# Expert products of a mixture layer: from split weights on the whole array to plain float32 on column quarters

## The chip, the cores and the metric

The kernel runs on one core of one Trainium2 chip. The metric is the device time of one execution in microseconds, from the first to the last instruction with what lies around it. All times in this document are of that one core. The engines are named as the profile names them: PE is TensorE (PEld its weight loads, PEldq its sequencer), ACT is ScalarE, DVE is VectorE, POOL is GpSimd and SP is SyncE, which here issues nearly all transfers.

## What is computed

A two-layer encoder trunk on 256 tokens of width 1024 in float32. Each layer has a mixer of four branches, a layer norm, a feed-forward part and another layer norm. The feed-forward part of the first layer is a dense SwiGLU; that of the second is a mixture of 8 experts, of which each token uses its two best. Everything that the change touches lies in that mixture:

```python
def swiglu(x, w1, w3, w2):
    return (jax.nn.silu(x @ w1) * (x @ w3)) @ w2

def moe_swiglu(x, router, w1, w3, w2):
    logits = jnp.einsum('bsd,de->bse', x.astype(jnp.float32), router.astype(jnp.float32))
    top_logit, top_idx = lax.top_k(logits, TOP_K)
    top_w = jax.nn.softmax(top_logit, axis=-1)
    gate = jnp.sum(jax.nn.one_hot(top_idx, N_EXPERTS, dtype=jnp.float32) * top_w[..., None], axis=-2)
    gate = gate.astype(x.dtype)
    out = jnp.zeros_like(x)
    for e in range(N_EXPERTS):
        out = out + gate[..., e:e + 1] * swiglu(x, w1[e], w3[e], w2[e])
    return out
```

An expert's w1 and w3 are 1024 x 3584 and its w2 is 3584 x 1024, so the eight experts have 352 MB of weights, and each is read once. The result has to hold float32 accuracy.

## The kernel before

The kernel sends only the tokens of an expert through it. The router (L716 to L743) takes the logits of all tokens, the two best experts of each, and the place of each token in each of its experts. A one-hot matrix of places times the tokens (`gather`, L805) gives `xe`, the tokens of two experts at a time, 128 places each. An expert that has more than `CAP` = 128 tokens would be finished in a second pass behind the branch at L959, which these inputs don't take.

Products are made in a fast format that holds less than float32. So each operand is split into a high and a low part: ScalarE copies a half block of weights into the fast format (`high`, L134), VectorE subtracts that from the original (`low`, L138), and `mm3` (L165) adds three products: high by high, high by low, low by high. The tokens are the stationary operand, 128 at a time, and the weights stream past them 512 columns wide, always over the full array of 128 x 128.

The weights come in blocks of 1 MB, 42 for each expert: 28 with columns of w1 and w3 side by side, 14 with rows of w2. SP fetches them (`fetch`, L114, the transfer at L118) into a ring of 15 places. The order of the 336 blocks is `order` (L635): two blocks of w1 and w3, which give 256 hidden columns, then the w2 block that belongs to the hidden columns two units earlier. Fourteen blocks are asked for ahead of the router, and three more ahead of the load of the count (below).

The loop over blocks is `steps` (L919), and the program order on each engine is written by hand: a step issues a block's 12 products (`first` for w1 and w3, `second` for w2), then SwiGLU (`act`, L587 and L588), then the split of the halves of later blocks (`half`), then what is due (`at`): the turn of a hidden chunk by two transposes (L845) and its split (L162, L163), the add of the finished expert (L878 to L880, one-hot places times results, scaled by the gate and added to `acc`), and the gather of the next two experts (L811). The accumulators are four banks `mm` for first products, gathers and adds, two banks `s` for second products, and two `tr` for turns. The count of the fullest expert (`over`, L897) is loaded to all engines ahead of the loop. The final norm (L216 to L232) and the output (L987) follow.

Elsewhere in the kernel, at L471 in the latent attention, products are made in plain float32, with 32 tokens on each of four quarters of the array's columns.

Of the kernel before, what the change touches and what calls it, by code (L numbers as in the profile page):

```python
# [36 lines left out]
LAG = 2  # L37
NW = 5
NR2 = 2
# [33 lines left out]
def trunk(tc, A, out):  # L73
# [8 lines left out]
    lnp = pool("ln", bufs=1)  # L82
    zp = pool("z", bufs=1)
# [24 lines left out]
    xh = cst.tile([128, 2, 8, 128], F32R, name="xh")  # L108
    xl = cst.tile([128, 2, 8, 128], F32R, name="xl")
# [18 lines left out]
    class Split:  # L128
# [3 lines left out]
        def high(self, raw, h):  # L132
            self.w.append([wp.tile([128, 1024], F32R, name=k)[:, :self.n] for k in ("wh", "wl")])
            nc.scalar.activation(self.w[h][0], raw[:, h * self.n:(h + 1) * self.n], AF.Copy)  # L134
# [500 lines left out]
    order = []  # L635
    for j in range(FFE // 256 + LAG):
        order += [2 * j, 2 * j + 1] * (j < FFE // 256) + [28 + j - LAG] * (j >= LAG)
    moe_raw = []

    def moe_fetch(n):  # L640
        return fetch(A["wmoe"][0, order[n]], zp, f"z{n}")

    def moe(xs, gb):
        with tc.tile_pool(name="moe", bufs=1, reuse_waits="tile") as ep:
            nj = FFE // 256
# [4 lines left out]
            places = [(zp, f"z{n}", None) for n in range(NZ)] + [(rawp, "raw", None)] * 4 + [(ep, "raw2", NR2)] * NR2  # L650
            first_places = list(places)
            places[1:1] = [(lnp, "gb", None), (xp, "x", None)]
            ring = len(places)

            def prefetch(i, p, tag, n):
                ready[0, order[i]] = fetch(src[0, order[i]], p, tag, n)

            def block(e, i):

                if (e, i) in ready:  # L660
                    return ready.pop((e, i))
                late = e * NU + order.index(i) - NE * NU
                if places[count[0] % ring][1] == "gb" and late > -36:
                    count[0] += 1
                raw = fetch(src[e, i], *places[count[0] % ring], parts=2 if late >= -2 else 1)
                count[0] += 1
                return raw

            for n in range(NZ, ring - 2):
                prefetch(n, *first_places[n])  # L670
            prefetch(len(first_places), ep, "ey", None)
            for n in range(NZ):
                ready[0, order[n]] = moe_raw[n]
            first_parts = []

            steps = [(e, i) for e in range(NE) for i in order]
            raws, parts = {}, {}

            def high(n, h):
                if h == 0:  # L680
                    raws[n], parts[n] = block(*steps[n]), Split()
                parts[n].high(raws[n], h)

            def low(n, h, eng=None):
                parts[n].low(raws[n], h, eng)

            def half(q, eng=None):

                high(q // 2, q % 2)
                low(q // 2, q % 2, eng)  # L690
# [8 lines left out]
            xT = ep.tile([128, 2, 8, 128], F32, name="rxT", tag="xe")  # L699
# [8 lines left out]
            flat = lambda a, t: a[:, t].rearrange("p k c -> p (k c)")  # L708
# [13 lines left out]
            def by_token(t):  # L722
                lgT = ep.tile([NE, 128], F32, name="lgT", tag="fs", bufs=2)
# [21 lines left out]
            def places_of(e, off, oh=None, ts=(0, 1)):  # L745

                oh = ep.tile([128, 2, 256], F32R, name="ohe") if oh is None else oh
                for t in ts:
                    for i in range(2):
                        nc.vector.tensor_scalar(oh[:, t, i * 128:(i + 1) * 128], iota, off + 1.0,  # L750
                                                pos[:, t, e + i:e + i + 1], op0=ALU.add, op1=ALU.is_equal)
                return oh

            pw = mm.tile([128, 512], F32, name="mm")
# [3 lines left out]
            half(0)  # L758
            for t in range(2):
                xs.begin(t)  # L760
            high(0, 1)
            high(1, 0)
            x.append(xs(0))
            x.append(xs(1))
            scopy(flat(xh, 0), x[0])
# [3 lines left out]
            nc.vector.tensor_tensor(flat(xl, 0), x[0], f(flat(xh, 0)), op=ALU.subtract)  # L769
            two(0, lg0)  # L770
            spin(pw[:, 0:128], 2)
            place(0)
            oh = places_of(0, 0, ts=(0,))
            scopy(flat(xh, 1), x[1])
            lg1 = by_token(1)
            low(0, 1)
            spin(pw[:, 0:128], 2)
            two(1, lg1)
            spin(pw[:, 0:128], 2)
            place(1)  # L780
            places_of(0, 0, oh, (1,))
            nc.vector.tensor_tensor(flat(xl, 1), x[1], f(flat(xh, 1)), op=ALU.subtract)
            low(1, 0)
            for q in range(3, NW):
                half(q)
            for t in range(2):
                nc.scalar.mul(x[t], x[t], ALPHA)
# [5 lines left out]
            acc = x  # L793
            sums = ep.tile([128, 2, 2], F32, name="sums")

            def weights(*_):
                nc.vector.tensor_scalar(w1, w2, 1.0, None, op0=ALU.add)
                nc.vector.reciprocal(w1, w1)
                nc.vector.tensor_tensor(w2, w2, w1, op=ALU.mult)
                for t in range(2):  # L800
# [346 lines left out]
```

## Time and profile before

| | us |
|---|---|
| median of 3 runs (lowest, highest) | 1680.96 (1678.39, 1681.54) |
| the profiled execution | 1681.01 |
| its span, first to last instruction | 1678.9 |
| of it up to the router | 657 |
| router and first gather | 21 |
| experts | 982 |
| last add, final norm, output | 18 |

One page of the profile sums up one execution: busy time of each engine, a picture of the span in 40 slices, queues, waits and the costliest groups of instructions. "Busy" of TensorE is modelled from pipelined records. A product in plain float32 leaves two weight loads and two MATMUL records, one in the fast format a single pair. [...] A row of waits names the engine and tile that waited, and what came last. The views behind the router are the ones that matter here.

### The profile page before, as it was taken

The numbers are of one execution on the slowest core, as the hardware profiler recorded it, in microseconds if no ns is written. First come the engines' busy times: TensorE is split into PE (matmuls) and PEld (weight loads), VectorE is DVE, ScalarE is ACT, GpSimd is POOL, SyncE is SP. The second block draws the span as 40 slices with busy tenths as digits, with TensorE's granted clock in tenths as the row PEclk, the third lists the DMA queues.
The fourth block names the chain that finished last, engine by engine and source line by source line (L and its number), as shares of the span: only waits on it lengthen the run. The fifth ranks groups of instructions, "written<-read, shape, count | busy, mean of one in ns | idle before, by whom it ended". The sixth has DMA issues, their size and how long they took to land. (4 is left out here: it accounts for less than half of the span.)

```text
span 1678.9 us, 21171 instructions
## 1 busy us (share of the span) xinstructions
PE 1648.5 (98%) x7783; PEld 1332.3 (79%) x7783; DVE 1380.9 (82%) x1834; ACT 1112.1 (66%) x1466; POOL 25.7 (2%) x29
## 2 busy tenths in 40 slices
PE   8999999999999999999999999999999999999996
PEld 7687878888868787888888888888888888888884
DVE  7688585554868858898988989998989988989986
ACT  4556645443455664777777777777777777777774
POOL 1000000000100000000000000000000000000000
PEclk9999999999999999999999999999999999999998
DMA  9344546555544655899999899999999999999860
GB/s 348 136 150 171 185 169 209 176 179 197 191 169 155 238 190 191 332 332 373 353 369 350 337 370 370 354 356 352 351 366 363 345 378 342 350 369 369 345 245 27
DMA packets 66928, 467.99 MB, mean 279 GB/s; under 512 B 7552, under 2 KB 8192, under 8 KB 11264
## 3 DMA queue, kind: packets, MB, share of 16 engines
q1 hardware_dynamic: 66816, 466.55, 74.8%
q8 instruction: 63, 1.03, 0.3%
q14 instruction: 49, 0.40, 0.1%
HBM read 465.48 MB, written 1.05 MB: 278 GB/s over the span
## 5 line engine op out<-in xcount | busy, mean ns | idle before, releaser
L138 DVE TENSOR_TENSOR wl<-raw,wh 128x1024 fp32r<-128x1024 f32 x870 | 1015.8, 1217 | 196.9 <-ACT wh L134 192.4
L134 ACT ACTIVATE wh<-raw 128x1024 fp32r<-128x1024 f32 x870 | 879.6, 1053 | 234.8 <-PE mm L170 201.4
L170 PE MATMUL mm<-wh,xe 128*128 128x512 f32 x1792 | 525.7, 397 | 0.0
L170 PEld LDWEIGHTS mm<-wh,xe 128*128 128x128 f32 x1792 | 328.5, 188 | 67.4
L170 PE MATMUL s<-wh,eh 128*128 128x512 f32 x896 | 299.8, 396 | 0.0
L170 PE MATMUL mm<-wl,xe 128*128 128x512 f32 x896 | 278.8, 392 | 0.0
L170 PEld LDWEIGHTS s<-wh,eh 128*128 128x128 f32 x896 | 168.7, 188 | 38.7
L170 PEld LDWEIGHTS mm<-wl,xe 128*128 128x128 f32 x896 | 168.1, 188 | 37.9
L587 ACT ACTIVATE fs<-mm 128x256 f32<-128x256 f32 x134 | 51.6, 385 | 206.7 <-PE mm L170 206.7
L170 PE MATMUL mm<-wh,xh 128*128 128x512 f32 (+2 forms) x592 | 183.2, 390 | 2.1 <-ACT xh L162 2.1
L170 PE MATMUL mm<-wh,xl 128*128 128x512 f32 (+2 forms) x592 | 179.2, 386 | 0.0
L170 PE MATMUL mm<-wl,xh 128*128 128x512 f32 (+2 forms) x592 | 178.6, 384 | 0.0
L170 PE MATMUL s<-wl,eh 128*128 128x512 f32 x448 | 177.0, 395 | 0.0
L170 PEld LDWEIGHTS mm<-wh,xh 128*128 128x128 f32 x592 | 108.5, 189 | 25.3 <-ACT xh L162 4.1
L170 PEld LDWEIGHTS mm<-wl,xh 128*128 128x128 f32 x592 | 109.2, 189 | 22.5 <-issue 0.8
L170 PEld LDWEIGHTS mm<-wh,xl 128*128 128x128 f32 x592 | 108.2, 189 | 22.1 <-issue 1.5
L170 PEld LDWEIGHTS s<-wl,eh 128*128 128x128 f32 x448 | 84.6, 189 | 18.8
L588 DVE TENSOR_TENSOR fs<-mm,fs 128x256 f32<-128x256 f32 x134 | 56.7, 423 | 36.2 <-ACT fs L587 35.9
L519 DVE SCALAR_TENSOR_TENSOR ac<-ud,smc,ac 128x256 f32<-128x256 f32 x120 | 53.2, 480 | 0.7
L163 DVE TENSOR_TENSOR eh<-tr,eh 128x256 fp32r<-128x256 f32 x112 | 46.8, 418 | 0.0
L162 ACT ACTIVATE eh<-tr 128x256 fp32r<-128x256 f32 x112 | 41.2, 368 | 4.5 <-PE tr L845 4.2
L845 PE MATMUL tr<-ident,fs 128*128 128x128 f32 x224 | 42.6, 272 | 0.0
(212 smaller groups left out, 1187.5 us busy)
## 6 DMA issues: line engine op xcount, KB each, us to landing
raw<-wmoe SPq DMA_DIRECT2D x334, 1024.0 KB, 6.4
raw<-wpre SPq DMA_DIRECT2D x95, 1024.0 KB, 4.9
gb<-lnp SPq DMA_DIRECT2D x5, 1024.0 KB, 5.8
raw<-wpre SPq DMA_DIRECT2D x4, 704.0 KB, 5.8
z<-biasB SPq DMA_DIRECT2D x8, 256.0 KB, 2.7
raw<-wmoe SPq DMA_DIRECT2D x4, 512.0 KB, 7.2
z<-cw SPq DMA_DIRECT2D x2, 640.0 KB, 6.6
x<-x SPq DMA_DIRECT2D x2, 512.0 KB, 3.9
```

Source lines behind the costliest of these rows:

```text
L134: nc.scalar.activation(self.w[h][0], raw[:, h * self.n:(h + 1) * self.n], AF.Copy)
L138: (eng or nc.vector).tensor_tensor(wl, raw[:, h * self.n:(h + 1) * self.n], f(wh), op=ALU.subtract)
L162: nc.scalar.activation(hi, src, AF.Copy)
L163: (eng or nc.vector).tensor_tensor(lo, src, f(hi), op=ALU.subtract)
L170: nc.tensor.matmul(ps, o[i], o[j], start=start and q == 0 and k == 0, stop=stop and q == 2 and k == n - 1)
L519: later.append(lambda c=c, k=k, w=w: nc.vector.scalar_tensor_tensor(ac[:, c], ud[:, c, k:k + S], w(k), ac[:, c], op0=ALU.mult, op1=ALU.add))
L587: nc.scalar.activation(s, ps[:, 0:256], AF.Silu)
L588: nc.vector.tensor_tensor(s, ps[:, 256:512], s, op=ALU.mult)
L845: nc.tensor.transpose(tr[:, i], s[:, i * 128:(i + 1) * 128], ident)
```

## The change

The experts' products are made in plain float32, so the weights need no split. The tokens of an expert are cut into tiles of 32. A tile is the stationary operand of one quarter of the array's columns, and the weights stream past it. Four chunks of 512 columns (256 of w1 and 256 of w3) are handled at once, one on each quarter: `quad(0)` to `quad(2)` of 8 blocks each, and `quad(3)` of 4 blocks with two chunks, so that two tiles share a bank. `second(q)` spreads the second products over the quarters in a like way, by the table `TASKS`. The order of blocks changes to match: first all of a quad, later its w2 blocks, and the last two w2 blocks of an expert behind the first eight of the next.

How many tiles an expert has is known only on the chip. The router counts the tokens of each expert (`cnt`), makes a class of 0 to 3 of it (`arm`: over 32, over 64, over 96), and TensorE loads the eight classes as registers. `arms` then writes each set of products four times, for 1 to 4 tiles, and two compares choose one. Only TensorE branches on the class. There are six sets for each expert. Banks without a tile get zeros by a product with a zero matrix, so that the other engines do the same work for any class. The products of a block wait for that block inside the arm; a place of the ring comes free when the arm has run its last products.

The gather is made for one expert at a time in float32. `acc` is a tile of its own. The ring has 21 places. Fifteen of its blocks are asked for ahead of the load of the count, which all engines make behind the router, and the rest behind it.

```diff
+            places = [(zp, f"z{n}", None) for n in range(NZ)] + [(rawp, "raw", None)] * 4
+            places += [(xhp, "xh", None), (xhp, "xl", None)]
+            places += [(wp, "w", None)] * NW + [(ep, "raw2", NR2)] * NR2
+            early = NZ + 4
...
+            order = []
+            for e in range(NE):
+                order += [(e, n) for n in range(8)] + [(e - 1, n) for n in (40, 41) if e]
+                order += [(e, n) for n in range(8, 40)]
+                order += [(e, n) for n in (40, 41) if e == NE - 1]
...
+            nc.vector.tensor_copy(cnt, pc)
+            nc.vector.tensor_scalar(arm, cnt, 32.5, None, op0=ALU.is_gt)
+            for c in (64.5, 96.5):
+                nc.vector.scalar_tensor_tensor(arm, cnt, c, arm, op0=ALU.is_gt, op1=ALU.add)
+            nc.vector.tensor_copy(armi, arm)
...
+            _, sel = nc.values_load_multi_w_load_instructions(armi[0:1, 0:NE], engines=[PE], min_val=0, max_val=3)
+            over = nc.values_load(mosti[0:1, 0:1], min_val=0, max_val=S)
...
+                        def body(b):
+                            for fn in fns:
+                                fn(b)
+                        v = sel[self.e]
+                        with tc.If(v < 2) as c:
+                            with tc.If(v < 1) as d:
+                                body(1)
+                            with d.Else():
+                                body(2)
+                        with c.Else():
+                            with tc.If(v < 3) as d:
+                                body(3)
+                            with d.Else():
+                                body(4)
...
+                def quad(self, q, lo=0, hi=8):
+                    def products(b):
+                        for k in range(lo, hi):
+                            if q < 3:
+                                w = self.w[8 * q + k]
+                                todo = [(self.ps[q][r][32 * c:32 * c + 32], r, w[:, c * 512:(c + 1) * 512])
...
+                            for ps, r, wc in todo:
+                                nc.tensor.matmul(ps, self.xe[:, k, 32 * r:32 * r + 32], wc, start=k == 0, stop=k == 7)
...
+                for e in range(NE + 1):
+                    x_ = None
+                    if e < NE:
+                        x_ = Expert(e, oh, xe)
+                        x_.blocks(*range(8))
+                        x_.quad_places(0)
+                        x_.arms(x_.quad(0))
+                    if last:
+                        last.blocks(40, 41)
+                        last.arms(last.second(3))
+                        last.evacuate()
+                    if e == NE:
+                        break
+                    x_.act(0)
+                    if e + 1 < NE:
+                        oh = places_of(e + 1, 0)
+                    x_.blocks(*range(8, 16))
+                    x_.quad_places(1)
+                    x_.turn_places(0)
+                    x_.arms(x_.quad(1))
+                    x_.turn(0)
+                    x_.turned(0)
+                    x_.act(1)
+                    if last:
+                        last.add()
+                    x_.second_places()
+                    x_.blocks(*range(16, 24), *range(28, 32))
+                    x_.quad_places(2)
+                    x_.turn_places(1)
+                    x_.arms(x_.quad(2), x_.second(0))
+                    x_.turn(1)
+                    x_.turned(1)
+                    x_.act(2)
+                    if e + 1 < NE:
+                        xe = gather(oh)
+                    x_.blocks(*range(24, 28), *range(32, 36))
+                    x_.quad_places(3)
+                    x_.turn_places(2)
+                    x_.arms(x_.quad(3), x_.second(1))
+                    x_.turn(2)
+                    x_.turned(2)
+                    x_.act(3)
+                    x_.blocks(*range(36, 40))
+                    x_.turn_places(3)
+                    x_.where_places()
+                    x_.turn(3)
+                    x_.turned(3)
+                    x_.arms(x_.where, x_.second(2))
+                    x_.wheres()
+                    if e == NE - 1:
                         gt = gb()
-                ex[NE - 1].add((0, 0), (0, 1))
+                    last = x_
+                last.add((0, 0), (0, 1))
 
                 with tc.If(over > CAP):
```

On TensorE, a unit of three blocks stood as this in the program before: products of two blocks of w1 and w3, of one of w2 (`s`), with a turn (`tr`) among them.

```order
L170 MATMUL s<-wl,eh 128x512
L170 MATMUL s<-wh,eh 128x512 x2
L170 MATMUL s<-wl,eh 128x512
L170 MATMUL s<-wh,eh 128x512
L170 MATMUL mm<-wh,xe 128x512 x2
L170 MATMUL mm<-wl,xe 128x512 x2
L170 MATMUL mm<-wh,xe 128x512 x4
L170 MATMUL mm<-wl,xe 128x512 x2
L170 MATMUL mm<-wh,xe 128x512 x2
L845 MATMUL tr<-ident,fs 128x128 x2
L170 MATMUL mm<-wh,xe 128x512 x2
L170 MATMUL mm<-wl,xe 128x512 x2
```

Now the same engine comes to `quad(0)` of the first expert so, behind the gather (L788): the load of the classes, two compares, and all four arms behind each other (32, 64, 96 and 128 products; `zero` fills the idle banks).

```order
L788 MATMUL tr<-oh,x 128x128 x16
L848 TENSOR_LOAD armi
L877 COMPARE_AND_BRANCH
L878 COMPARE_AND_BRANCH
L908 MATMUL mm<-raw,xe 32x512 x4
L913 LDWEIGHTS zero
L913 MATMUL mm<-zero 128x512
L913 LDWEIGHTS zero
L913 MATMUL mm<-zero 128x512
L913 LDWEIGHTS zero
L913 MATMUL mm<-zero 128x512
L908 MATMUL mm<-raw,xe 32x512 x28
```

These are the compares and the arm for one tile. The end of the same set, from the products of the arm for two tiles on, stands so, and the next set follows:

```order
L908 MATMUL mm<-raw,xe 32x512 x56
L878 UNCONDITIONAL_BRANCH
L883 COMPARE_AND_BRANCH
L908 MATMUL mm<-raw,xe 32x512 x12
L913 LDWEIGHTS zero
L913 MATMUL mm<-zero 128x512
L908 MATMUL mm<-raw,xe 32x512 x84
L883 UNCONDITIONAL_BRANCH
L908 MATMUL mm<-raw,xe 32x512 x128
L883 UNCONDITIONAL_BRANCH
L848 ISA x16
L877 COMPARE_AND_BRANCH
```

What stood as 12 products for each block, one after the other, is now a choice of four stretches that lie behind each other, of which three are jumped over.

On SP, which issues the transfers, the fetches of blocks (`wmoe`) around the router stood so, with the load of the count (`mosti`) behind three of them:

```order
L118 DMA raw<-wpre 128x2048 x9
L118 DMA raw<-wmoe 128x2048 x7
L694 DMA rt<-router 128x64
L118 DMA raw<-wmoe 128x2048 x3
L897 TENSOR_LOAD mosti
L897 ISA x2
L118 DMA raw<-wmoe 128x2048 x303
```

Now the load stands behind seven:

```order
L118 DMA raw<-wmoe 128x2048
L721 DMA rt<-router 128x64
L118 DMA raw<-wmoe 128x2048 x7
L849 TENSOR_LOAD mosti
L849 ISA x2
L118 DMA raw<-wmoe 128x2048
L877 UNCONDITIONAL_BRANCH
L118 DMA raw<-wmoe 128x2048 x4
L877 UNCONDITIONAL_BRANCH
L118 DMA raw<-wmoe 128x2048 x13
```

With the eight that stand further up, 15 blocks are asked for ahead of the load, where it was 17; the fetches behind it are cut by a jump at the end of each set, one for each set of arms (L877).

## Rows read from the trace of the kernel before

**Rows 1.** the page's first part: busy us, share of the span, instructions

```profile
PE 1648.5 (98%) x7783; PEld 1332.3 (79%) x7783; DVE 1380.9 (82%) x1834; ACT 1112.1 (66%) x1466; POOL 25.7 (2%) x29
```

**Rows 2.** windows of the end: busy us of engines, granted clock, DMA share, GB/s

```profile
core 0: us, PE busy (x) PEld busy (x) DVE busy (x) ACT busy (x) POOL busy (x), PEclk, DMA share, GB/s
657.00:668.00 11.00, 7.87 (x62) 5.83 (x61) 8.93 (x21) 5.58 (x11) 0.92 (x1) 1.00 0.01 1
668.00:678.40 10.40, 8.77 (x39) 8.12 (x39) 8.44 (x18) 5.89 (x8) 0.00 (x0) 0.51 0.76 303
678.40:1660.60 982.20, 982.20 (x4427) 800.71 (x4425) 890.57 (x994) 746.36 (x929) 0.00 (x0) 1.00 0.91 342
...
1664.80:1679.00 14.20, 2.04 (x4) 1.16 (x4) 7.88 (x18) 3.04 (x8) 2.50 (x2) 0.50 0.20 76
```

**Rows 3.** the same view, 240 us from the middle of the experts

```profile
980.00:1220.00 240.00, 240.00 (x1087) 195.94 (x1086) 219.43 (x246) 182.97 (x229) 0.00 (x0) 1.00 0.95 357
```

**Rows 4.** the page's costliest groups: busy, mean ns, idle ahead of them

```profile
L138 DVE TENSOR_TENSOR wl<-raw,wh 128x1024 fp32r<-128x1024 f32 x870 | 1015.8, 1217 | 196.9 <-ACT wh L134 192.4
L134 ACT ACTIVATE wh<-raw 128x1024 fp32r<-128x1024 f32 x870 | 879.6, 1053 | 234.8 <-PE mm L170 201.4
```

**Rows 5.** waits in 678 to 1661, ScalarE's and the fetching queue's: us, times, longest

```profile
ACT fs L587 <- PE mm L170: 188.8, 112, 2.4
...
SPq L118 <- DVE wl L138: 806.6, 318, 6.2
```

**Rows 6.** TensorE's timeline in the router and late in the experts: start, length

```profile
657.05 1.03 PE L716 MATMUL tr<-ident,x 128*128 128x128 f32 x8
658.54 1.91 PE L720 MATMUL s<-rxT,rt 128*8 128x128 f32 x16 [0.45 <-ACT rxT L755]
...
1606.07 0.38 PE L845 MATMUL tr<-ident,fs 128*128 128x128 f32 x2
...
1614.61 0.38 PE L845 MATMUL tr<-ident,fs 128*128 128x128 f32 x2
```

**Rows 7.** the page's transfers: count, size, median us from issue to landing

```profile
raw<-wmoe SPq DMA_DIRECT2D x334, 1024.0 KB, 6.4
```

**Rows 8.** L471: all of its records, then of one part of it, windows, timeline

```profile
L471 PE MATMUL mm<-z x96: 482/507/617, 66.1 to 490.1; 128*32 128x512 f32 x32, 128*32 128x384 f32 x32, 64*32 64x384 f32 x32
L471 PEldq EVENT_SEMAPHORE  x2: 51/51/51, 64.0 to 481.8; - x2
...
L471 PE MATMUL mm<-z x46: 482/496/617, 485.7 to 490.1; 128*32 128x384 f32 x16, 64*32 64x384 f32 x16, 128*32 128x512 f32 x14
...
L471 PE MATMUL mm<-z x12: 482/592/617, 487.7 to 488.6; 128*32 128x512 f32 x8, 64*32 64x384 f32 x4
...
488.10:488.98 0.88, 0.88 (x12) 0.29 (x12) 1.00 0.01 5
...
485.69 4.90 PE L471 MATMUL mm<-z 128*32 128x512 f32 x46
```

**Rows 9.** L959, a jump of each engine's sequencer in ns, and the instruction queue

```profile
L959 PEldq COMPARE_BRANCH  x1: 3738/3738/3738, 1662.6 to 1662.6; - x1
L959 DVEq COMPARE_BRANCH  x1: 72/72/72, 1663.1 to 1663.1; - x1
...
q8 instruction: 63, 1.03, 0.3%
```

**Rows 10.** groups of the expert stage, small work: busy, mean ns, idle ahead

```profile
L588 DVE TENSOR_TENSOR fs<-mm,fs 128x256 f32<-128x256 f32 x112 | 47.5, 424 | 31.1 <-ACT fs L587 30.8
...
L587 ACT ACTIVATE fs<-mm 128x256 f32<-128x256 f32 x112 | 43.2, 385 | 188.8 <-PE mm L170 188.8
...
L880 DVE SCALAR_TENSOR_TENSOR x<-mm,egate,x 128x512 f32<-128x512 f32 x28 | 20.9, 745 | 0.0
L878 PE MATMUL mm<-ey,ohT 128*128 128x512 f32 x29 | 11.8, 407 | 0.0
...
L163 DVE TENSOR_TENSOR ey<-s,ey 128x512 fp32r<-128x512 f32 x15 | 10.0, 687 | 2.8 <-ACT ey L162 2.8
```

More of the change, by code (lines that the diff above doesn't have):

```diff
@@ L669, in moe @@
[L669 to L682, printed above, removed]
@@ L693, in moe @@
+            def block(e, i):
+                while (e, i) not in ready:
+                    fetch_next()
+                return ready.pop((e, i))
+            for n in range(early):
+                fetch_next()
             rt = ep.tile([128, 8, NE], F32, name="rt")
@@ L858, in second @@
-                def second(self, j, w):
-                    if j == 0:
-                        self.py = [sps.tile([128, 512], F32, name="s") for _ in range(2)]
-                    h = self.h.pop(j)
-                    for k in range(2):
-                        for half in range(2):
-                            mm3(self.py[half], [(h[:, 0, k], h[:, 1, k], *w.at(k * D + half * 512, 512))],
-                                j == 0 and k == 0, j == nj - 1 and k == 1)
+                    self.ps, self.s, self.tr, self.h, self.w, self.py = {}, {}, {}, {}, {}, None
@@ new lines, in second_places, with second, products @@
+                def second_places(self):
+                    self.py = [sps.tile([128, 512], F32, name="s") for _ in range(2)]
+                def second(self, q):
+                    def products(b):
+                        n = 8 if q < 3 else 4
+                        for k, half, r, g, first, last in TASKS[b]:
+                            if not 8 * q <= k < 8 * q + n:
+                                continue
+                            c, f_ = k // 2 % 4, k % 2
+                            if q < 3:
+                                i, cc = r, 32 * c
+                            else:
+                                i, cc = r // 2, 32 * (2 * (r % 2) + c)
+                            w = self.w[28 + k // 2]
+                            o = f_ * D + half * 512
+                            nc.tensor.matmul(self.py[half][32 * g:32 * g + 32],
+                                             self.h[q][i // 2][:, i % 2, f_, cc:cc + 32], w[:, o:o + 512],
+                                             start=first, stop=last)
+                    return products
@@ new lines, in where_places, with where @@
+                def where_places(self):
+                    self.wtr = trp.tile([128, 2, 2, 128], F32, name="tr")
+                def where(self, b):
+                    for half in range(2):
+                        for t in range(2):
+                            for g in range(4):
+                                r = BINS[b][half][g]
+                                nc.tensor.matmul(self.wtr[32 * g:32 * g + 32, half, t], self.oh[:, t, 32 * r:32 * r + 32],
+                                                 ident, start=True, stop=True)
@@ L886, in moe @@
-            gather(xe, oh, range(8))
-            weights()
-            region.close()
-            pc = sps.tile([128, NE], F32, name="s")
-            for t in range(2):
-                nc.tensor.matmul(pc, tri[:, 1], selb[:, t], start=t == 0, stop=t == 1)
-            most = ep.tile([128, 1], F32, name="most")
-            nc.vector.tensor_reduce(most, pc, axis=AX.X, op=ALU.max)
-            mosti = ep.tile([128, 1], I32, name="mosti")
-            nc.vector.tensor_copy(mosti, most)
-            over = nc.values_load(mosti[0:1, 0:1], min_val=0, max_val=S)
@@ L979, in moe @@
                 norms[0].spread(sums[:, 0])
[L980 removed]
+                last.add((1, 0), (1, 1))
                 norms[1].spread(sums[:, 1])
```

356 lines of the change are left out of this document (177 added, 179 removed).

## The prediction

> **What bounds the kernel now.** The profiled execution took 1681.01 us, 2.11 us more than its span of 1678.9 us, and its own time stands 0.05 us above the median of the three runs; every sum below is made for that execution. I first read the totals of the page: TensorE is busy 98% of the span [rows 1]. Then the stages. The change touches only what lies behind the router, so the windows matter: in the expert stage, 678.4 to 1660.6, TensorE is busy for all 982.20 us at a granted clock of 1.00, VectorE 890.57, ScalarE 746.36 [rows 2]. So TensorE sets the end there, and nothing that it waits for does: ScalarE waits for it 112 times, 188.8 us in all, while the fetching queue waits 806.6 us for VectorE's second halves of the splits, that is, for places to put weights [rows 5]. The turns of two neighbouring units of three blocks start at 1606.07 and 1614.61, 8.54 us apart [rows 6]; 112 such units make 956 us of the 982.
>
> The second bound is close. In 240 us of the middle the DMA engines are busy 0.95 of the time and move 357 GB/s [rows 3]; at a full share that would be 376 GB/s, or 2.8 us for a block of 1 MB, so three blocks need 8.4 us against 8.54. No faster arithmetic can bring the stage below the weights: 336 blocks at 2.8 us are 941 us.
>
> **What goes.** The splits of the expert weights: 672 of the 870 halves of ScalarE's L134 (1053 ns) and VectorE's L138 (1217 ns) [rows 4], 708 and 818 us. Neither sets the end now, so by itself this is worth nothing; it leaves both engines nearly empty. The fp32r products, 12 for a block of which 36 fill most of a unit, go too.
>
> **What comes: products.** A group is four plain fp32 products 512 columns wide, one on each quarter of the array's columns. The kernel has such products in its latent attention, at L471. Between 488.10 and 488.98 two sets of four records run, one group (a product leaves two records), and take 0.88 us [rows 8]. The upper end is the whole run of 46 records in 4.90 us [rows 8]: 14 of them are 512 wide and 32 are 384 wide, 19,456 columns, so 4,096 columns cost 1.03 us with the last record's drain in it. I take 0.88, as the arms run much longer than 46 records and pay the drain once.
>
> The reference's router, on its inputs, gives the experts 61, 32, 101, 73, 49, 83, 23 and 90 tokens, so b, the number of 32-token tiles, is 2, 1, 4, 3, 2, 3, 1, 3. An expert needs 42 groups for each tile, and 4 more where b is odd (a half of the last quad stays idle): 84, 46, 168, 130, 84, 130, 46, 130, in sum 818 groups or 720 us. Before, each expert cost 42/3 times 8.54, 120 us, whatever its count. An expert of four tiles now takes 148 us of products and falls behind its 42 x 2.8 = 118 us of weights; one of three, 114 us, is level with them; those of one and two tiles are well ahead.
>
> **Loads, experts 0 and 1.** SP now asks for 15 blocks ahead of its load of the count, where 17 stood, and for four more behind it; the twentieth takes the place of the first, which comes free when quad 0 of expert 0 has run. That can begin where the first expert product began before, at 678.4 [rows 2]; 16 groups are 14 us and a jump some 4, so the twentieth is asked for near 696. Under a full stream a block lands 6.4 us after it is asked for [rows 7], alone it needs 2.8 for its bytes; I take 4, so 700. SP's wait for the count lies in front of that and costs nothing as long as it is over by then. Expert 1's last block but the two that are read later is number 82: 700 + 62 x 2.8 = 874. With two tiles and one, 130 groups or 114 us in some 195 us, TensorE waits for weights nearly all through, and small work and jumps there are hidden. Near 876 expert 2 begins (8 us either way).
>
> **TensorE, experts 2 to 7.** From there TensorE should be the later one. Products: 688 groups x 0.88 = 605 us. Small work of one expert: 28 turns at 0.13 (eight transposes take 1.03 us [rows 6]), 3.6 us; eight products of the add at 0.41 [rows 10], 3.3; the gather, now 16 fp32 products of 128 columns at 0.24 (eight of them, 16 records, take 1.91 us [rows 6]), 3.8; the transposed places and the zeros for idle banks, some 1.5. That is 12.2 us. Waits: ahead of quad 1 the accumulators must be read, after the last second products were (two halves at 0.69 on VectorE, then 0.385 on ScalarE and 0.424 on VectorE for the first bank [rows 10]), 3 us; adds wait for VectorE's 0.745 each [rows 10], behind four multiplications, 3; gather 1; the last turn of an expert, 2. That is 9 us, ends 4 and 15. Together 21.2 x 6 = 127, less what expert 7 lacks, 125. So 876 + 605 + 125 = 1606. The tail, from the end of the stage at 1660.6 [rows 2] to 1678.9, 18.3 us, stays: 1624. The last block could land at 700 + 316 x 2.8 = 1585, before TensorE needs it, so the loads do not set this end; with TensorE free of every cost the loads alone would give about 1588 + 18 + 2 = 1608.
>
> **Branches.** Every expert has six branch sets, and all four arms stand in the program, only one of which is run: some 1280 instructions for a quad. TensorE has run one long jump before, L959, and its sequencer took 3738 ns for it, where VectorE's took 72 [rows 9]. The instruction queue moved 63 packets in 1.03 MB, 16 KB each [rows 9], for the 15,566 records of TensorE [rows 1], the most of any engine; that is about 250 a packet, and five packets for a quad. Entries and exits of arms that lie further than the packet at hand and the next: I count 39 in experts 2 to 7. The sequencer runs ahead of its engine: at L471 it passed its wait at 64.0 where the first product starts at 66.1, 2.1 us [rows 8]. Of 3.74 us this hides 2.1 and leaves 1.64: 39 x 1.64 = 64 us. Ends: 0, if the lead is larger in long arms, and 39 x 3.74 = 146, if every jump begins with an empty queue. I take the middle, since L471 is the nearest row that shows a lead.
>
> [...]
>
> **The clock.** After the small steps of the router the granted clock was 0.51 for 10.4 us, with TensorE busy 8.77 of them, and then 1.00 for all 982 us of unbroken products [rows 2]; in the thin work of the tail it was 0.50 [rows 2]. Such a spell costs 10.4 x 0.49 = 5.1 us. Jumps and waits break up what was unbroken; I take one spell for each of experts 2 to 7, 31 us, with ends 0 and two for each, 61.
>
> **The sum.** 1624 + 64 + 31 = 1719 as span, 2 more as time: about **1721 us**, 40 us above the kernel before. In bounds: jumps -64 to +82, clock -31 to +30, a group at 1.03 instead of 0.88 +103, waits -30 to +36, start -8 to +8.
>
> **Rivals.** *The jumps are covered* (faster). The sequencer's lead grows in arms of hundreds of records, and a jump falls where TensorE has to wait for a bank anyway; then little of the 64 and perhaps of the 31 is left: 1626 with both gone, 1657 with the clock's share left; 1677 is the point from which it is no longer faster, that is 51 of the 95 us exposed. For it: the 9 us of waits and the jumps lie at the same places. Against: at a wait the sequencer stands still, so it has no lead behind one.
>
> *Everything is exposed* (slower still). All 39 jumps stand in the open with 3.74 us, and the gaps bring a second spell of half clock in each expert: 1721 + 82 + 30 = 1833.
>
> *The quarters do not run side by side when their streams differ.* At L471 all four read the same operand; here each quarter has its own 512 columns. Were they to run two and two, a group would cost 1.76: TensorE sets the end from 678 on, 678 + 818 x 1.76 + 8 x 21 + 18, near 2304. The records of L471 show four starts at one time, but not this case.
>
> *The change does not do what it says*: the counts choose too large an arm. With four tiles for all, 1344 groups x 0.88 give some 2050 us. The order of the branch rules that out as far as it can be read, and I give it no more than a share of the next line.
>
> **Chances.** Forecast 0.58, with 0.53 for slower and 0.05 for within 0.2% (3.4 us, about what a measurement of this kernel tells from no change); covered jumps 0.31, faster; all exposed 0.08; quarters or arms not as thought 0.03. So faster 0.31, same 0.05, slower 0.64. The range reaches from 1640, into the middle of the first rival, to 1800, near the second: below 1640 I leave some 0.10, above 1800 some 0.10. The forecast's own range is 1678 to 1785.
>
> **What would show it.** Right: rows of a long compare-and-branch or jump on TensorE's sequencer of about 3.7 us, five to eight for an expert, with TensorE idle 1 to 2 us behind each; granted clock under 1.00 in windows of experts 2 to 7; groups of eight 512-wide records each 0.88 us inside an arm; the DMA share at 0.95 in experts 0 and 1 and below that in the later ones; the fetching queue waiting for TensorE. Wrong: TensorE never idle behind a jump (first rival), or the DMA share at 0.95 to the end, which would put the time at 1608 to 1626; a group over 0.95 us would move the whole sum up by 7 us for each hundredth.

## The result: 15% slower, and the profile after

| | us |
|---|---|
| before, median (4 runs) | 1681.25 |
| after, median of 4 runs (lowest, highest) | 1934.43 (1932.58, 1939.54) |
| ratio, 95% interval | 1.1514 (1.1487 to 1.1541) |
| span of the profiled execution | 1933.9 |

The forecast was slower, at 1721 with a range of 1640 to 1800. The direction held, the size did not: the kernel lost 253 us, and the forecast had 40.

The page of the changed kernel answers to [rows 1, 9]. Its slices are 48 us each; the experts fill those from the fifteenth on.

```profile
PE 1584.0 (82%) x10539; PEld 843.2 (44%) x10539; DVE 572.1 (30%) x1070; ACT 426.2 (22%) x704; POOL 25.0 (1%) x29
...
PE   8999999999999968685668787877857786766886
...
PEclk9999999999999989797889897988878888778888
DMA  8344455555456596998544574467785449996430
...
q8 instruction: 208, 3.41, 0.7%
```

Three things are new in the experts. TensorE, which had no idle time there, is busy five to eight tenths. Its granted clock (PEclk, in tenths of full speed) is under nine tenths in 21 of the 26 slices. And the instruction queue moved 208 packets (3.41 MB) where it moved 63. ScalarE and VectorE are nearly idle there, as forecast.

Windows by stage, with the columns of [rows 2]: experts 0 and 1, experts 2 to 7, the tail.

```profile
672.00:903.80 231.80, 161.59 (x1208) 59.06 (x1210) 20.94 (x57) 21.35 (x48) 0.00 (x0) 0.84 0.94 383
903.80:1914.70 1010.90, 760.32 (x5990) 254.81 (x5990) 70.47 (x177) 50.72 (x131) 0.00 (x0) 0.85 0.61 248
1914.70:1933.90 19.20, 4.18 (x16) 1.83 (x8) 10.52 (x24) 4.12 (x10) 1.84 (x2) 0.64 0.16 58
```

Against the prediction's sum: expert 2 begins at 903.8 and not 876, 28 us late; experts 2 to 7 take 1010.9 and not 730 + 95 = 825, 186 us more; the tail is 19.2 against 18.3. That is the whole miss of 215 us in the span, and 186 of it lie in one stage, experts 2 to 7. There TensorE is idle for 250.6 us, at a granted clock of 0.85, with the weights at 248 GB/s and a share of 0.61: neither arithmetic nor loads set the end.

The compares and jumps of TensorE's sequencer, as in [rows 9] (the line's x, then shortest, median and longest in ns):

```profile
L877 PEldq COMPARE_BRANCH  x48: 65/164/8236, 670.1 to 1906.3; - x48
...
L878 PEldq COMPARE_BRANCH  x48: 65/4563/6774, 670.3 to 1772.6; - x48
...
L883 PEldq COMPARE_BRANCH  x42: 65/312/7915, 898.1 to 1912.5; - x42
...
L1053 PEldq COMPARE_BRANCH  x1: 3501/3501/3501, 1917.7 to 1917.7; - x1
```

L1053 is the old L959; it takes 3.5 us, where it took 3.7. The new ones go up to 8.2. Counted one by one, 53 jumps of over 1 us lie in experts 2 to 7, 294.5 us together, 5.6 each. One of them, and TensorE around it:

```profile
L883 PEldq COMPARE_BRANCH  x1: 6291/6291/6291, 1184.2 to 1184.2; - x1
```

```profile
1164.27 3.64 PE L908 MATMUL mm<-raw,xe 128*32 128x512 f32 x16 [4.05 <-issue]
...
1168.38 18.56 PE L908 MATMUL mm<-raw,xe 128*32 128x512 f32 x168
1190.57 1.97 PE L931 MATMUL tr<-ident,fs 128*128 128x128 f32 x8 [3.62 <-issue]
1192.37 0.79 PE L992 MATMUL tr<-ey,ohT 128*128 128x512 f32 x1
...
1202.27 5.44 PE L908 MATMUL mm<-raw,xe 128*32 128x512 f32 x24 [4.88 <-issue]
```

The same two jumps as windows, with the columns of [rows 2]:

```profile
1184.22:1190.51 6.29, 2.73 (x28) 0.58 (x20) 0.00 (x0) 0.00 (x0) 0.00 (x0) 0.93 1.02 429
1195.98:1201.97 5.99, 1.40 (x4) 0.61 (x2) 1.51 (x4) 0.00 (x0) 0.00 (x0) 0.50 1.01 417
```

The jump out of the arm starts at 1184.2, while TensorE still has 2.7 us of products in its queue, and takes 6.29; so 3.62 us of idle time with nothing to wait for ("issue"). The next jump, into an arm, leaves 4.88. Beside both the stream of weights keeps the transfer engines full (1.02 and 1.01). In the second window the granted clock is at 0.50, and behind it 24 records, three groups, take 5.44 us at 1202.27, 1.8 a group. Ahead of the first gap 21 groups take 18.56 us (the 168 records at 1168.38, at a granted clock of 0.98), 0.88 each.

### The profile page after: what moved, and what is told of

Same layout as the page of the kernel before. It is cut to its first block, busy times and chain, and to the rows that moved or that the text cites. A ratio compares the mean times of both kernels' runs of the same rounds, so it can differ in the third digit from the quotient of the medians.

```text
span 1933.9 us, 24487 instructions
## 1 busy us (share of the span) xinstructions
PE 1584.0 (82%) x10539; PEld 843.2 (44%) x10539; DVE 572.1 (30%) x1070; ACT 426.2 (22%) x704; POOL 25.0 (1%) x29
## 3 DMA queue, kind: packets, MB, share of 16 engines
q8 instruction: 208, 3.41, 0.7%
## 5 line engine op out<-in xcount | busy, mean ns | idle before, releaser
L908 PE MATMUL mm<-raw,xe 128*32 128x512 f32 x4256 | 533.7, 632 | 164.0 <-issue 117.2
L908 PEld LDWEIGHTS mm<-raw,xe 128*32 128x32 f32 x4256 | 143.7, 115 | 521.1 <-issue 458.5
L171 PE MATMUL mm<-w,xh 128*128 128x512 f32 (+2 forms) x1184 | 314.1, 386 | 1.7 <-ACT xh L163 1.7
L960 PE MATMUL s<-raw,eh 128*32 128x512 f32 x2128 | 265.9, 635 | 40.0 <-issue 40.0
L139 DVE TENSOR_TENSOR w<-raw,w 128x1024 fp32r<-128x1024 f32 (+1 forms) x198 | 238.2, 1207 | 135.7 <-ACT w L135 135.0
L135 ACT ACTIVATE w<-raw 128x1024 fp32r<-128x1024 f32 (+1 forms) x198 | 206.3, 1047 | 197.9 <-PE mm L171 170.6
L171 PEld LDWEIGHTS mm<-w,xh 128*128 128x128 f32 x1184 | 215.9, 189 | 45.7 <-ACT xh L163 3.8
L171 PE MATMUL mm<-w,xl 128*128 128x512 f32 (+2 forms) x592 | 178.2, 384 | 0.0
L960 PEld LDWEIGHTS s<-raw,eh 128*32 128x32 f32 x2128 | 78.2, 117 | 213.8 <-issue 210.1
L171 PEld LDWEIGHTS mm<-w,xl 128*128 128x128 f32 x592 | 108.3, 189 | 21.5 <-issue 1.5
L922 DVE TENSOR_TENSOR fs<-mm,fs 128x256 f32<-128x256 f32 x112 | 39.7, 413 | 11.5 <-ACT fs L921 11.5
L788 PE MATMUL tr<-oh,x 128*128 128x128 f32 x256 | 41.2, 332 | 2.3 <-issue 1.6
L788 PEld LDWEIGHTS tr<-oh,x 128*128 128x128 f32 x256 | 39.1, 244 | 4.7 <-ACT eh L941 2.3
```

The costliest lines, as they stand in the source:

```text
L139: (eng or nc.vector).tensor_tensor(wl, raw[:, h * self.n:(h + 1) * self.n], f(wh), op=ALU.subtract)
L171: nc.tensor.matmul(ps, o[i], o[j], start=start and q == 0 and k == 0, stop=stop and q == 2 and k == n - 1)
L788: nc.tensor.matmul(ps[:, i], x[t][:, k * 128:(k + 1) * 128], oh[:, t], start=t == 0, stop=t == 1)
L908: nc.tensor.matmul(ps, self.xe[:, k, 32 * r:32 * r + 32], wc, start=k == 0, stop=k == 7)
L922: nc.vector.tensor_tensor(s, ps[:, 256:512], s, op=ALU.mult)
L960: nc.tensor.matmul(self.py[half][32 * g:32 * g + 32], self.h[q][i // 2][:, i % 2, f_, cc:cc + 32], w[:, o:o + 512], start=first, stop=last)
```

## Experiments

A time that stands here without an interval is that of a single execution.

**Is it the branches at all?** The first run writes the counts of these inputs into the program.

```diff
-                        v = sel[self.e]
-                        with tc.If(v < 2) as c:
-                            with tc.If(v < 1) as d:
-                                body(1)
...
+                        body((2, 1, 4, 3, 2, 3, 1, 3)[self.e])
```

> The changed kernel without its branches: the number of tiles of each expert is written into the program for these inputs (2, 1, 4, 3, 2, 3, 1, 3), so TensorE has one stretch where four stood; it computes the whole result, but would be wrong for other inputs. Theory (the jumps are the loss): of experts 2 to 7, 1010 us in the changed kernel, the 195 us go in which TensorE stood idle in a long jump, most of the 51 us of products at half clock, and the late start of expert 2 (28 us): 1934 - 195 - 40 - 25, about 1675, between 1630 and 1700. Rival (the pace of the new order: waits between the stages, half clock from thin work, whatever the branches do): over 1800.

1583.36 us, ratio to before 0.9417 (0.9402 to 0.9433). The rival is out: without its branches the changed kernel is 6% faster than before, and the branches, with the arms that they pass over, cost 351 us. Its windows for the same three stages:

```profile
672.00:844.40 172.40, 144.19 (x1202) 49.08 (x1206) 21.07 (x57) 20.44 (x47) 0.00 (x0) 0.93 1.01 421
844.40:1564.20 719.80, 681.72 (x5994) 229.94 (x5986) 70.39 (x177) 50.73 (x131) 0.00 (x0) 0.98 0.91 369
1564.20:1583.30 19.10, 4.13 (x16) 1.83 (x8) 10.53 (x24) 4.13 (x10) 1.84 (x2) 0.65 0.16 58
```

Side by side with the changed kernel: 59.4 us are lost in experts 0 and 1, 291.1 in experts 2 to 7, nothing in the tail. Of the 291, idle time of TensorE is 250.6 - 38.1 = 212.5, and nearly the same records (5990 and 5994) are busy 760.3 instead of 681.7 us, 78.6 more. Most of that is the clock, 0.85 against 0.98: by the trace's records of it TensorE is busy for 171 us at half clock here and for 23 us without branches, and half of the difference is 74. My expectation of 1675 was 92 us too high: experts 0 and 1 gained 59 and not 25, the clock gave back 79 and not 40, and the idle time 212 and not 195.

**How far is far?** Behind each set of products of that kernel stands a stretch that never runs (no class is over 3), of a different length in each expert. A product is four instructions.

```diff
+                        far = (8, 16, 32, 64, 96, 128, 192, 256)[self.e]
+                        v = sel[self.e]
+                        with tc.If(v < 4) as c:
+                            body(b)
+                        with c.Else():
...
+                            for _ in range(far):
+                                nc.tensor.matmul(ps[0:32], self.xe[:, 0, 0:32], self.w[max(self.w)][:, 0:512], start=True, stop=True)
```

> As the run without branches, but behind each set of products stands a stretch that is never run and has to be jumped over: 8, 16, 32, 64, 96, 128, 192 and 256 products of four instructions in experts 0 to 7, six times each. It computes the whole result. Theory (a jump is dear only where its target isn't among the instructions at hand): under some length a jump costs next to nothing, above it 3 to 7 us, with a step somewhere from 250 to 500 instructions, that is between 64 and 128 products. Rival (any taken jump empties what was fetched): 3 to 7 us for all of them.

1666.71 us. The line's rows in windows of the experts 0 to 7, in order; each holds the compares, at 65 to 80 ns, and four or five jumps:

```profile
L879 PEldq COMPARE_BRANCH  x9: 65/169/188, 683.0 to 752.8; - x9
...
L879 PEldq COMPARE_BRANCH  x8: 65/124/312, 780.2 to 844.5; - x8
...
L879 PEldq COMPARE_BRANCH  x8: 65/124/292, 903.6 to 1001.0; - x8
...
L879 PEldq COMPARE_BRANCH  x7: 65/286/1606, 1054.1 to 1134.7; - x7
...
L879 PEldq COMPARE_BRANCH  x7: 65/407/6143, 1176.5 to 1239.7; - x7
...
L879 PEldq COMPARE_BRANCH  x7: 65/3272/6172, 1306.1 to 1399.7; - x7
...
L879 PEldq COMPARE_BRANCH  x7: 65/5918/6305, 1436.4 to 1493.7; - x7
...
L879 PEldq COMPARE_BRANCH  x7: 65/3318/4525, 1555.2 to 1636.8; - x7
```

| products jumped over (instructions) | the six jumps, us |
|---|---|
| 8, 16, 32 (32 to 128) | 0.17 to 0.38, all 18 |
| 64 (256) | 0.28, 0.29, 0.30, 0.79, 1.61, 4.13 |
| 96 (384) | 0.30, 0.41, 0.52, 5.99, 6.14, 6.14 |
| 128 (512) | 3.27, 4.45, 5.58, 6.06, 6.17, 6.21 |
| 192 (768) | 5.92 to 7.10, all six |
| 256 (1024) | 6.02, 4.53, then 3.32 to 3.71 |

Length decides, with a soft step between 256 and 512 instructions, as the theory had it. Each length stands in an expert of its own, so the lengths were met at different times; but the cheap jumps of experts 0 to 2 ran beside a stream of 333 to 421 GB/s (the page's slices from 666 to 1040), so no idle stream made them cheap. The last four jumps over 1024 instructions are cheaper than those over 768: by then the weights have all landed (a DMA share of 0.01 to 0.02). (The 3.27 in the row of 512 fell into a pause of the stream, at a share of 0.02.)

**Why 6 us and not 3.7?** The next run keeps the branches and leaves out the loads behind the first 19 blocks; its products read those again.

```diff
+                if n >= len(first_places):
+                    ready[e, i] = kept[n % len(first_places)]
+                    return
```

> The changed kernel with all its branches, but only the first 19 of the 336 weight blocks are fetched; the later products read these again. It leaves out the loads, so its result is not the reference's. Theory (a jump is dear because its code has to come through transfer engines that are full of weights): long jumps fall from some 6 us to the 3.3 to 3.7 us that L1053 and the last two long ones show with the engines idle. Rival (the price is that of the code jumped over, whatever else is moved): they stay near 6 us. Time by the theory about 1610 to 1680 (818 groups at 0.88, small work, and 66 jumps of 3.5 of which 2 us each lie hidden), by the rival above 1750.

1711.77 us. The jumps, and one of them as a window with its idle transfer engines (a share of 0.02):

```profile
L882 PEldq COMPARE_BRANCH  x48: 65/162/5183, 671.2 to 1683.7; - x48
...
L883 PEldq COMPARE_BRANCH  x48: 65/1098/3869, 671.4 to 1556.9; - x48
...
L888 PEldq COMPARE_BRANCH  x42: 65/355/5159, 847.0 to 1688.3; - x42
```

```profile
706.02:709.56 3.54, 2.72 (x28) 0.58 (x20) 0.00 (x0) 0.00 (x0) 0.00 (x0) 1.00 0.02 5
```

One by one, 49 of 59 jumps over 1 us now take 3.0 to 3.9 us, and eight take 4.7 to 5.2, mostly where one follows another at once; none reaches 6, where those of the changed kernel are mostly 5.5 to 8.2. The median is 3.5 us here and 6.0 in the changed kernel. So the price has two parts: some 3.5 us for the jump, and some 2.5 more for the transfer engines being full. The trace's records of the instruction queue show where these 2.5 us lie: the first packet of code starts 0.98 us into a long jump here, and 3.48 us into one beside the stream (medians of 58 and 61 jumps of 2.5 us and more); the packet itself takes some 1.0 us in both, and some 1.4 us pass behind it. The code waits before it moves. The time was above my 1610 to 1680. The same without branches:

> Neither branches nor, after the first 19 blocks, loads; it leaves out the loads, so its result is not the reference's. TensorE alone: 678 + 720 + 8 x 21 + 18, less what the waits do not reach, 1520 to 1590. Beside the run without the stream but with branches (1711.8) it gives the price of the branches with idle transfer engines: theory, 59 jumps of 3.6 us each less a lead of about 2, 95 to 130 us, and some half clock, in all 110 to 170; rival (the branches disturb otherwise than by the jumps): over 200.

1547.93 us, and the rival is out. So the branches cost 164 us with idle transfer engines and 351 with the stream of weights (1934.4 - 1583.4): the stream more than doubles them. Nearly the same packets of code came in both: 205 without the stream, 208 with it, against 84 and 85 without branches, about two for each long jump, of which mostly one starts during the jump.

**Smaller packets of weights?** The changed kernel again, with each later block of weights in four transfers.

```diff
-                    ready[e, i] = fetch(src[e, i], *first_places[n])
+                    ready[e, i] = fetch(src[e, i], *first_places[n], parts=4)
...
-                    ready[e, i] = fetch(src[e, i], *places[count[0] % ring], parts=2 if n >= len(order) - 2 else 1)
+                    ready[e, i] = fetch(src[e, i], *places[count[0] % ring], parts=4)
```

> The changed kernel, but each block of weights from the twelfth on is fetched in four transfers of 512 columns, so rows of 2 KB where they were 8 KB. It computes the whole result. With the transfer engines idle a long jump took 3.3 to 3.7 us, with the stream of weights 5.7 to 6.5. Theory (the code waits in turn behind single packets of weights, so smaller ones let it through sooner): long jumps under the stream fall to 4 to 5 us and the time by 50 to 100 us, to 1830 to 1890. Rival (the code waits for its share of engines that are full, whatever the packets' size, or behind all that was asked for before it): jumps stay at 6 us and the time at 1925 to 1945.

1953.43 us, no gain: the theory falls, and the time lies 8 us above the rival's range too. Windows of 80 us in expert 1, changed kernel first, then this one, and one line of its jumps:

```profile
820.00:900.00 80.00, 53.53 (x359) 22.07 (x359) 8.83 (x22) 6.34 (x16) 0.00 (x0) 0.83 1.01 417
```

```profile
820.00:900.00 80.00, 57.58 (x349) 23.46 (x341) 8.93 (x22) 6.34 (x16) 0.00 (x0) 0.84 1.02 356
...
L878 PEldq COMPARE_BRANCH  x48: 65/4292/7607, 671.0 to 1786.2; - x48
```

Engines that are full with rows of 2 KB move 356 GB/s, with rows of 8 KB 417, and the jumps stay at 6 us (the median of those over 1 us is 6.0 in both). What the code waits behind is left open; shorter rows did not shorten the wait.

**A version without long jumps.** Tiles 0 and 1 of a quad run without a branch; tiles 2 and 3 stand behind, 128 instructions each, and are skipped. The second products stand in sets of four steps, with arms of 16, 24 and 32 products.

```diff
+                def quads(self, q):
+                    self.quad(q, rs=range(2))
+                    v = sel[self.e]
+                    with tc.If(v < 2) as c:
...
+                    with c.Else():
+                        self.quad(q, rs=(2,))
+                        with tc.If(v < 3) as d:
...
+                        with d.Else():
+                            self.quad(q, rs=(3,))
```

> The same products, but the branches rearranged so that no jump is long; it computes the whole result for any counts. Tiles 0 and 1 of a quad run without a branch, the products of tile 2 and of tile 3 (32 products, 128 instructions each) stand behind and are skipped where there is no such tile; the second products stand in sets of 4 steps with three arms of 16, 24 and 32 products. An expert of one tile is handled as one of two. Theory (only long jumps are dear, and the loss of the changed kernel is theirs): all jumps pass at most 256 instructions and cost 0.1 to 1.6 us, mostly inside TensorE's lead; time that of the run without branches, 1583, plus up to 33 us for expert 6 with two tiles, plus 10 to 40 us: 1595 to 1655, faster than both kernels. Rival (code comes at some 6 us for a packet under the load of weights, so passing code costs as well as jumping over it): experts of two tiles, which pass 15 packets in 74 us of products, starve, and the time stays over 1680.

> The kernel of short jumps with its branches replaced by these inputs' counts (2, 2, 4, 3, 2, 3, 2, 3 tiles); it computes the whole result, but would be wrong for other inputs. Both theories: 1583 to 1620, the bound of the kernel of short jumps; the difference between the two is what its branches and the code passed cost, by the theory under 40 us, by the rival 60 or more.

1719.12 us (ratio to before 1.0216, 1.0191 to 1.0242) and 1617.11 for its bound: 102 us for branches, of which each passes 256 instructions at most. The theory missed here, and the rival was right about the place:

```profile
L877 PEldq COMPARE_BRANCH  x96: 65/216/6164, 716.7 to 1687.9; - x96
...
L880 PEldq COMPARE_BRANCH  x56: 65/198/4952, 980.0 to 1692.7; - x56
...
L905 PEldq COMPARE_BRANCH  x48: 65/210/5916, 685.0 to 1655.3; - x48
...
L910 PEldq COMPARE_BRANCH  x28: 65/202/324, 906.4 to 1660.6; - x28
```

Of the 33 jumps over 1 us, 120 us together, 22 are at L877, out of the arm for two tiles, eight at L880, out of that for three, and three at the quads (L905). In an expert of two tiles the program passes 288 instructions of second products while it runs 16 products of them, four groups or 3.5 us, set after set. The reading that fits is that a short jump is cheap only when the code behind it has had time to come; the next run puts it to the test.

**Less code to pass.** The second products of tiles 0 and 1 always run, in one bank for both halves of the result, and those of tiles 2 and 3 go to the other and are skipped; the add gets four products of 64 rows.

```diff
+                def seconds(self, q):
+                    self.second(q, 2)
+                    v = sel[self.e]
+                    with tc.If(v > 1) as c:
+                        with tc.If(v < 3) as d:
+                            self.second(q, 3)
+                        with d.Else():
+                            self.second(q, 4)
```

> As the kernel of short jumps, but with less code to pass: tiles 0 and 1 of the second products always run, in one accumulator for both halves of the result, and tiles 2 and 3 stand behind in the other, to be skipped; the add has four products of 64 rows where it had two of 128. It computes the whole result for any counts. An expert of two tiles passes 728 products of code where it passed 952. Theory (what was left of the loss in the kernel of short jumps, 102 us above its bound, is code that doesn't come fast enough for experts of one and two tiles): 1617 + 25 for the longer add + 20 to 60, so 1660 to 1700. Rival (it is the number of branches, 229 there and about as many here, that costs): 1720 to 1750.

1644.28 us, ratio 0.9781 (0.9765 to 0.9798). That is below the 1660 to 1700 of the theory, and far from the rival's. The rival isn't wholly out, as the branches fell too, from 229 to 156, and this kernel was not run without its branches; but those under 1 us take 0.07 to 0.3 mostly, and of the dear ones, 33 with 120 us, eight with 21 us are left:

```profile
L905 PEldq COMPARE_BRANCH  x48: 65/210/6162, 683.9 to 1586.3; - x48
...
L910 PEldq COMPARE_BRANCH  x28: 65/176/314, 882.0 to 1591.6; - x28
...
L965 PEldq COMPARE_BRANCH  x32: 67/142/3223, 724.5 to 1621.6; - x32
...
L966 PEldq COMPARE_BRANCH  x32: 67/178/646, 964.4 to 1623.3; - x32
```

The same with weights in rows of 2 KB:

> The same with weights in rows of 2 KB. By the theory on small packets 10 to 40 us below the same kernel with rows of 8 KB; by its rival the same within 5 us, or some slower if the stream loses speed.

1706.97 us: 63 us slower. The stream falls to some 290 to 360 GB/s, at a share of 0.86 to 1.02, so the loads, it seems, set the end again.

**One tile.** Where an expert has one tile, tile 1 of quads 0 to 2 is skipped too.

```diff
+                    self.quad(q, rs=(0,))
+                    with tc.If(v < 1) as c:
+                        zeros(1, 2, 3)
+                    with c.Else():
+                        self.quad(q, rs=(1,))
+                        rest()
```

> The kernel of pairs, but tile 1 of quads 0 to 2 is skipped too where an expert has one tile (experts 1 and 6), which jumps over 96 products or 384 instructions; tile 0 runs alone ahead. It computes the whole result for any counts. Of 384 instructions three jumps of six were dear in the run of lengths. Theory (the jump costs 6 us less some 2.5 of lead in about half of the cases, the products that go are 24 groups or 21 us in expert 6; expert 1 waits for weights): 1644 - 21 + 6, about 1630, between 1620 and 1645. Rival (tile 0 alone ahead makes TensorE wait for the last block of each quad where loads are late, and the code passed grows no less): no gain, 1645 to 1665.

1634.43 us, ratio to before 0.9727 (0.9709 to 0.9744). All six jumps over 384 instructions were dear, 1.5 to 6.1 us each (26 in sum), three of them in expert 1, and the time still fell by 10 us, so the products that went were worth more. This is the fastest kernel of the study that is written for any counts: 46 us below the kernel before, 300 below the change as made, and 51 above the one that knows its counts.

## Why the prediction was wrong

- **Products: right.** 0.88 us a group holds (the 21 groups at 1168.38 above), and the quarters run side by side with different streams. Products, small work and waits of experts 2 to 7 were 605 + 125 = 730; without branches they take 719.8.
- **Loads, experts 0 and 1: the start failed twice, in opposite directions.** The stream was priced at 2.8 us a block, from 357 GB/s at a share of 0.95 [rows 3]. With the places free it moves 421 GB/s at 1.01, 2.5 us a block, and without branches expert 2 begins at 844.4, not 876. The floor of 941 us for 336 blocks falls with that price: without branches the experts take 892 us, 672.0 to 1564.2. And "small work and jumps there are hidden" was wrong: with branches it begins at 903.8, 59 us later. A place comes free when its arm is through, so a late arm stops the queue. Fetches waited for TensorE 132 us in that stage (first two of these rows) and 13 without branches (the last two):

```profile
SPq L118 <- PE mm L908: 90.8, 35, 22.2
...
SPq L118 <- PE s L960: 41.6, 15, 20.0
```

```profile
SPq L118 <- PE mm L898: 12.5, 11, 2.6
SPq L118 <- PE s L950: 0.7, 3, 0.3
```

- **Branches: the step that failed.** That long jumps would leave TensorE idle was right (250.6 us of idle time in experts 2 to 7, 38.1 without branches), the term 39 x (3.74 - 2.1) = 64 us was not; 53 x (5.6 - 1.9) = 195 us stood open in its place. The number was 53, not 39: how far a jump has to go to be a long one was an estimate of mine, for which no row of the kernel before stood, and the run of lengths puts the step between 256 and 512 instructions. The price was 5.6, not 3.74. The lead came out near the forecast, 294.5 - 195 us or 1.9 for each jump, but in part by luck: behind the end of an arm it is mostly 2.7 us (28 records, as at 1184.22), and nine jumps have none. Which of the 53 the count of 39 lacked was not sorted out. The price came from L959, the one long jump of the kernel before, which ran at 1662.6, when the transfer engines were at a share of 0.04 (the row below). The new ones run beside a full stream. A row for the price was taken from a place where the resource that sets it is idle. The run without the stream shows it: 3.0 to 3.9 us again for most.

```profile
1660.60:1664.80 4.20, 1.61 (x4) 0.59 (x4) 2.63 (x6) 0.57 (x1) 0.00 (x0) 0.99 0.04 10
```

- **Two jumps in a row** were each given a lead of their own. Where an arm's exit, v < 2 and v < 3 come behind each other, the second and third have none: 16.31 us of idle time before 953.49, with three jumps from 933.8 on.

```profile
953.49 29.63 PE L908 MATMUL mm<-raw,xe 128*32 128x512 f32 x256 [16.31 <-issue]
```

- **The clock: too small.** 31 us, at most 61; it took some 79 more than without branches. The granted clock fell to half not once for each of the six experts but 35 times in all (7 times without branches). So the 186 us of this stage are 148 in idle time (212.5 instead of 64) and 48 in the clock, less 10 in products and waits.
- **The rivals.** "The jumps are covered" is out. The sentence against it, that there is no lead behind a wait, shows in the trace: at 818.81 and 1659.58 TensorE has stood for 2.54 and 2.55 us until VectorE's `fs` (L922) and starts its product 0.2 us after its sequencer's records of the wait, at 818.60 and 1659.37. "Everything is exposed", 1833, had the right direction and the same wrong price: it was thought to be a bound and was not one, since the price's upper end was the only row there was. The range should have had an end for a dearer jump.
- **The signs to look for** held in kind, not in size: DMA share of 0.94 in experts 0 and 1 and 0.61 later, long jumps (nine for an expert, not five to eight), idle time behind them (mostly 3 to 5 us, not 1 to 2), the queue waiting for TensorE.

## What to carry to other kernels

A branch is paid for by the code that it leaves out and by what else the transfer engines do: a jump over up to 128 instructions took TensorE's sequencer 0.2 to 0.4 us here where long stretches of products ran between the jumps, one over 512 and more some 3.5 with idle engines and 6 beside a full stream, of which TensorE's queue hid some 2. Short jumps in quick succession were dear as well: in the kernel of short jumps 33 took over 1 us, up to 6.2. So put the common part ahead without a branch, let the rare parts stand behind it as short stretches to be skipped, and keep all arms together small; done so, the same idea went from 15% slower to 3% faster. And when a price is taken from a trace, look at what else was running in that row.

## What the runs showed of the hardware

- Code comes in packets of 16 KB that the trace lists among the transfers (208 with 3.41 MB in the changed kernel, 85 without branches), about two for a long jump, and where the transfer engines are full it waits: a long jump took mostly 3.0 to 3.9 us with idle engines and mostly 5.5 to 8.2 with full ones, and its first packet started 0.98 and 3.48 us into the jump. Rows of 2 KB instead of 8 KB in the stream did not shorten it (the median of the jumps over 1 us is 6.0 in both).
- The stream of weights in rows of 8 KB runs at 417 to 421 GB/s on one core where its places are free, against 357 at a share of 0.95 in the kernel before [rows 3]; in rows of 2 KB at 356 in the 80 us shown above, where rows of 8 KB move 417. Why it was slower there was not tried.
